# Two attention groups open their value sums with their own first product, not with a product of the zero tile

## The chip, the cores and the metric

The kernel runs on one core of one Trainium2 chip. The metric is the device time of one execution in microseconds. TensorE (PE in the profile, PEld for its weight loads) multiplies matrices into PSUM, which has eight banks of 128 x 512 float32; VectorE (DVE), ScalarE (ACT) and GpSimd (POOL) do the rest; SyncE (SP) issues most DMAs.

## The reference

A trunk of two layers over 1024 tokens of width 1024, in float32. Each layer projects the normalised input once, feeds the pieces to four groups of attention heads (A latent attention, B differential attention, C windowed attention with sinks, D attention over a neighbourhood of the token grid), joins their outputs, projects them, and adds an MLP with squared ReLU.

```
for l in range(DEPTH):                                  # 2
    h = rms_norm(x, norm1_g[l])
    proj = h @ w_in[l]
    (a_cq, a_ckv, a_kr, b_q, b_k, b_v, c_q, c_k, c_v, d_q, d_k, d_v) = jnp.split(proj, splits, axis=-1)
    y_a = mla_mixer(...)
    y_b = diff_mixer(...)
    y_c = swa_mixer(c_q, c_k, c_v, swa_sinks[l], cos64, sin64)
    y_d = na_mixer(d_q, d_k, d_v, na_rpb[l])
    mix = jnp.concatenate([rms_norm(y_a, out_g_mla[l]), y_b,
                           rms_norm(y_c, out_g_swa[l]), rms_norm(y_d, out_g_na[l])], axis=-1)
    x = x + mix @ w_out[l]
    h = rms_norm(x, norm2_g[l])
    x = x + jnp.square(jax.nn.relu(h @ w_up[l])) @ w_down[l]
return rms_norm(x, final_norm_g)
```

In C and D each query sees only keys nearby. With blocks of 128 tokens (in D the tokens are reordered so that this holds too), the queries of block i meet the keys of blocks i-1, i and i+1 only.

## The kernel before

**The order.** The program doesn't issue instructions as it goes. Every call adds a step to a list (`Plan.add`), and when all are there, `Plan.order` works out the order of each engine's queue: it walks through a model of the engines, and at each moment takes the step with the earliest due time whose inputs are ready and for which a buffer can be granted. Due times come from `Plan.stream`: each stage has a span in `SPAN` (D from 230 to 390, C from 300 to 405, B from 65 to 330, the latents' projections "lat" from 270 to 325 and "up" from 335 to 390), and the span is shared out among the stage's steps by the price of its TensorE steps. So the stages interleave: D and C run beside B and the projections. Steps added inside `together` form one unit and are issued one behind the other. All real instructions are emitted in one place, so the profile gives all of them line 677.

**Groups D and C.** Both use `banded` (1450), two calls per group and layer, each for two heads with 64 value columns each. For block i, `score` makes the scores of both heads (TensorE into banks "sb"), and `finish` turns them into exponentials (VectorE, ScalarE). For key block kb, `parts` (1469) transposes the probabilities of up to three query blocks into a bank "tr" and copies them to SBUF as `pt`. `products` (1486) multiplies values by `pt` into a bank "pv": head 0 into partitions 0 to 63, head 1 into partitions 64 to 127. One bank holds half of the queries, four blocks of 128 columns; a product covers the columns of those query blocks that the key block meets, so neighbouring products overlap in columns. The first half takes key blocks 1, 0 and later 4, 3, 2; the second takes 4, 3 and later 7, 6, 5. When a half is complete, `pair_out` (1244) copies it with one ScalarE instruction.

**The zero product.** Since no product covers the whole bank, `zeroed` (1481) opens each bank with one product of the zero tile: 128 x 128 zeros times a broadcast column of zeros, 512 columns wide, with `start=True`. All real products then add (`start=False`). `zeroed` is called twice per `banded`, so eight times per layer. It depends on nothing but a free bank. Groups A and B (`dense`, 1306) don't use it: there, products cover equal columns and the first one carries `start=True`.

The zero tile is also multiplied `IDLE` = 12 times at the very start, into a bank that nobody reads, and VectorE reads it as an operand in `softmax`.

Of the kernel before, what the change touches and what calls it, by code (L numbers as in the profile page):

```python
# [23 lines left out]
P = 128  # L24
# [612 lines left out]
class Trunk:  # L637
# [812 lines left out]
    def banded(self, qs, ks, vs, y, finish, grid=False):  # L1450


        nc = self.nc
        mm = nc.tensor.matmul
        heads = [slice(j * 64, j * 64 + 64) for j in range(2)]
        tiles, done = {}, {}

        def score(i):
            p = tiles[i] = self.ptile()
            lo, hi = max(i - 1, 0), min(i + 1, 7)  # L1460
            w, s0 = (hi - lo + 1) * P, (lo - i + 1) * P
            ps = [self.bank("sb")[:, :w] for _ in heads]
            for b, q, k in zip(ps, qs, ks):
                for n in range(2):
                    mm(b, q[:, i * P:(i + 1) * P], k[n][:, lo * P:(hi + 1) * P], start=n == 0, stop=n == 1)
            for j, b in enumerate(ps):
                finish(j, b, p[:, j * 512 + s0:j * 512 + s0 + w], i)

        def parts(kb):

            i0, i1 = max(kb - 1, 0), min(kb + 1, 7)
            out = []
            for j in range(2):
                t = self.bank("tr")
                for i in range(i0, i1 + 1):
                    at = j * 512 + (kb - i + 1) * P
                    nc.tensor.transpose(t[:, (i - i0) * P:(i - i0 + 1) * P], tiles[i][:, at:at + P], self.ident)
                out.append(self.transposed(t[:, :(i1 - i0 + 1) * P]))
            done[kb] = out, i0, i1

        def zeroed():
            pv = self.bank("pv")
            mm(pv, self.zero, self.zero[:, 0:1].broadcast_to([P, 512]), start=True, stop=False)
            return pv

        def products(pv, half, kbs):
            with self.plan.together():
                for kb in kbs:
                    pts, i0, i1 = done[kb]
                    q0, q1 = max(i0, half * 4), min(i1, half * 4 + 3) + 1  # L1490
                    for r, v, pt in zip(heads, vs, pts):
                        mm(pv[r, (q0 - half * 4) * P:(q1 - half * 4) * P], v[:, kb],
                           pt[:, (q0 - i0) * P:(q1 - i0) * P], start=False, stop=kb == 2 + 3 * half)

        for i in range(self.ahead):
            score(i)
        yield True
        for kb in range(8):
            if kb + self.ahead < 8:
                score(kb + self.ahead)  # L1500
            parts(kb)
            if kb == 1:
                pv = zeroed()
                products(pv, 0, (1, 0))
            if kb == 4:
                products(pv, 0, (4, 3, 2))
                self.pair_out(pv, y, 0, grid)
                pv = zeroed()
                products(pv, 1, (4, 3))
            yield True  # L1510
        products(pv, 1, (7, 6, 5))
        self.pair_out(pv, y, 1, grid)
        yield True
# [494 lines left out]
```

## Time and profile before

| | |
|---|---|
| median of 3 runs | 2522.7 us |
| lowest and highest run | 2518.65 and 2522.78 us |
| the profiled execution, its own time | 2517.78 us |
| its span, first to last instruction | 2516.0 us |
| mean granted TensorE clock | 0.996 |
| TensorE busy | 2467.4 us (98%) |
| VectorE busy | 1909.8 us (76%) |
| ScalarE busy | 1290.5 us (51%) |

Durations are microseconds unless marked ns. A row of the groups has engine, operation, output and inputs, shapes, count, then busy time in total, mean ns of one, and the idle time of the engine just before them with what ended it. A row of the timeline has start, duration, engine, line, operation, shapes and count; a bracket at its end is the idle time before it and what ended that. A row of the chain of waits has start, duration and what the time went to; "x334" is a run of 334 instructions with nothing between. Matmuls overlap in the pipeline and their ends are modelled, so the distance between starts says more than the duration. A row of the busy time by stages has the stage, its length, the busy time of PE, PEld, DVE, ACT and POOL with instruction counts, the granted clock, the DMA share and GB/s.

### The profile page before, as it was taken

How to read it: one execution, taken by the hardware profiler on the slowest of the kernel's cores; microseconds unless marked ns; L12 is line 12 of the kernel's file. 1: busy time of each engine (PE TensorE's matmuls, PEld its weight loads, DVE VectorE, ACT ScalarE, POOL GpSimd, SP SyncE). 2: the span in 40 equal slices, each digit the busy share in tenths (PEclk: the TensorE clock that was granted, in tenths of full speed). 3: DMA queues.
4: the chain of work that ended last, by engine and by line, in shares of the span. 5: the costliest groups of instructions: out<-in, count | busy, mean ns of one | idle time of the engine just before them, and what ended most of it. 6: DMA issues, size and time to landing. Idle time of an engine off the chain costs nothing.

```text
span 2516.0 us, 35396 instructions
## 1 busy us (share of the span) xinstructions
PE 2467.4 (98%) x12332; PEld 1967.1 (78%) x12332; DVE 1909.8 (76%) x3576; ACT 1290.5 (51%) x2397; POOL 379.7 (15%) x258
## 2 busy tenths in 40 slices
PE   8999999999999999999999999999999999999998
PEld 6777776778888887888877777677788888888887
DVE  7767867775877779888777677677678777898887
ACT  4545757653644445444425456666455444444454
POOL 3323224213000000000042231332140000000000
PEclk9999999999999999999999999999999999999999
DMA  5534478622244457444154344885123444665431
GB/s 180 180 112 133 122 218 234 197 80 72 78 165 159 151 202 271 147 142 139 72 182 130 119 117 135 232 255 170 46 70 117 155 155 158 231 231 158 130 105 67
DMA packets 190514, 378.56 MB, mean 150 GB/s; under 512 B 24112, under 2 KB 36352, under 8 KB 190336
## 3 DMA queue, kind: packets, MB, share of 16 engines
q1 hardware_dynamic: 175360, 350.09, 44.6%
q10 hardware_dynamic: 14976, 26.22, 2.7%
q8 instruction: 97, 1.59, 0.3%
q14 instruction: 81, 0.66, 0.1%
HBM read 260.15 MB, written 116.07 MB: 150 GB/s over the span
## 4 chain that ended last, share of the span: by engine, by line
PE 83%; DVE 8%; DMA 4%; ACT 2%; issue 2%; SPq 1%; POOL 0%; DVEq 0%; POOLq 0%; ACTq 0%
PE bank L677 83%; DVE p L677 2%; DVE part L677 1%; SPq L677 1%; ACT p L677 1%; DVE x L677 1%; DMA a<-in_w_down 1%; DVE sq L677 1%; DMA acts<-ev 1%; DVE col L677 0%; DMA latp<-lat 0%; DMA c<-in_w_down 0%; DVE xl L677 0%; DVE ev L677 0%; DVE both L677 0%
## 5 line engine op out<-in xcount | busy, mean ns | idle before, releaser
L677 PE MATMUL bank<-far,wh 128*128 128x512 f32 (+1 forms) x2848 | 870.3, 387 | 1.1 <-ACT wh L677 0.6
L677 PEld LDWEIGHTS bank<-far,wh 128*128 128x128 f32 x2848 | 532.4, 188 | 110.5 <-ACT wh L677 1.4
L677 PE MATMUL bank<-far,wl 128*128 128x512 f32 (+1 forms) x1424 | 550.3, 387 | 2.7 <-DVE wl L677 2.7
L677 ACT ACTIVATE p<-p,col 128x1024 f32<-128x1024 f32 (+2 forms) x320 | 294.6, 921 | 196.3 <-DVE col L677 194.2
L677 POOL TENSOR_TENSOR wl<-ws,wh 128x512 fp32r<-128x512 f32 (+1 forms) x138 | 191.1, 1390 | 1180.2 <-ACT wh L677 1089.8
L677 PEld LDWEIGHTS bank<-far,wl 128*128 128x128 f32 x1424 | 267.4, 188 | 57.9 <-DVE wl L677 3.4
L677 PE MATMUL bank<-stack 96*128 96x512 f32 (+2 forms) x896 | 285.0, 395 | 5.0 <-DVE col L677 2.3
L677 DVE TENSOR_TENSOR x<-bank,x 128x512 f32<-128x512 f32 (+1 forms) x276 | 187.2, 680 | 121.9 <-PE bank L677 121.0
L677 PE MATMUL bank<-ident,p 128*128 128x128 f32 x1376 | 253.6, 276 | 10.4 <-DVE part L677 4.8
L677 PE MATMUL bank<-xh,wh 128*128 128x512 f32 x608 | 250.9, 413 | 3.1 <-ACT wh L677 2.6
L677 PE MATMUL bank<-xh,wl 128*128 128x512 f32 x608 | 250.6, 413 | 1.1 <-POOL wl L677 1.1
L677 PE MATMUL bank<-xl,wh 128*128 128x512 f32 x608 | 250.6, 412 | 0.0
L677 PEld LDWEIGHTS bank<-ident,p 128*128 128x128 f32 x1376 | 171.3, 141 | 59.5 <-issue 10.7
L677 PEld LDWEIGHTS bank<-stack 96*128 96x128 f32 (+1 forms) x896 | 159.3, 189 | 43.8 <-DVE col L677 12.1
L677 ACT ACTIVATE pt<-bank 128x512 f32<-128x512 f32 (+2 forms) x256 | 137.5, 556 | 82.9 <-PE bank L677 75.2
L677 DVE TENSOR_TENSOR wl<-raw,wh 128x512 fp32r<-128x512 f32 x224 | 150.3, 690 | 34.5 <-ACT wh L677 34.0
L677 PE MATMUL bank<-pt,v 128*64 128x256 f32 (+2 forms) x1344 | 173.1, 396 | 2.2 <-ACT pt L677 2.0
L677 ACT ACTIVATE ev<-ev 128x512 f32<-128x512 f32 x128 | 80.6, 632 | 160.3 <-DVE ev L677 155.8
L677 DVE CUSTOM_DVE_ANT_0 p<-bank,zero,col 128x512 f32<-128x512 f32 x192 | 143.8, 749 | 22.2 <-PE bank L677 5.1
L677 PE MATMUL bank<-mix,wh 128*128 128x512 f32 x512 | 160.3, 393 | 0.0
L677 DVE CUSTOM_DVE_ANT_0 p<-bank,zero 128x512 f32<-128x512 f32 x192 | 131.7, 686 | 35.4 <-PE bank L677 34.1
L677 ACT ACTIVATE wh<-raw 128x512 fp32r<-128x512 f32 x224 | 135.4, 621 | 23.8 <-ACT ev L677 10.5
(158 smaller groups left out, 3904.5 us busy)
## 6 DMA issues: line engine op xcount, KB each, us to landing
act<-acts SPq DMA_DIRECT2D x224, 256.0 KB
raw<-in_w_up SPq DMA_DIRECT2D x128, 256.0 KB
acts<-ev SPq DMA_DIRECT2D x128, 256.0 KB
acts<-ev ACTq DMA_DIRECT2D x96, 256.0 KB
ws<-in_w_in SPq DMA_DIRECT2D x76, 256.0 KB
c<-in_w_down SPq DMA_DIRECT2D x64, 256.0 KB
rz<-drows SPq DMA_DIRECT2D x40, 256.0 KB
ws<-in_w_out SPq DMA_DIRECT2D x40, 256.0 KB
```

The lines of the kernel that those rows point to most:

```text
L677: getattr(s.eng.engine, s.op)(*[real(a) for a in s.args], **{k: real(a) for k, a in s.kw.items()})
```

## The change

`zeroed` goes. The bank is taken where it was called, and the first key block of each half (1 in the first half, 4 in the second) multiplies with `start=True`, once for each of the two heads. Columns of the bank that this first product does not cover are reached by later products with `start=False`.

```diff
-        def zeroed():
-            pv = self.bank("pv")
-            mm(pv, self.zero, self.zero[:, 0:1].broadcast_to([P, 512]), start=True, stop=False)
-            return pv
-
         def products(pv, half, kbs):
             with self.plan.together():
                 for kb in kbs:
                     pts, i0, i1 = done[kb]
                     q0, q1 = max(i0, half * 4), min(i1, half * 4 + 3) + 1
                     for r, v, pt in zip(heads, vs, pts):
                         mm(pv[r, (q0 - half * 4) * P:(q1 - half * 4) * P], v[:, kb],
-                           pt[:, (q0 - i0) * P:(q1 - i0) * P], start=False, stop=kb == 2 + 3 * half)
+                           pt[:, (q0 - i0) * P:(q1 - i0) * P], start=kb == 1 + 3 * half,
+                           stop=kb == 2 + 3 * half)
...
             if kb == 1:
-                pv = zeroed()
+                pv = self.bank("pv")
                 products(pv, 0, (1, 0))
             if kb == 4:
                 products(pv, 0, (4, 3, 2))
                 self.pair_out(pv, y, 0, grid)
-                pv = zeroed()
+                pv = self.bank("pv")
                 products(pv, 1, (4, 3))
```

## The prediction

> **What bounds the kernel now.** I read the page's busy shares first, then its chain of waits, then the groups by form, and last the timeline of TensorE around each product of the zero tile.
>
> ```profile
> span 2516.0 us, 35396 instructions
> PE 2467.4 (98%) x12332; PEld 1967.1 (78%) x12332; DVE 1909.8 (76%) x3576; ACT 1290.5 (51%) x2397; POOL 379.7 (15%) x258
> PE 83%; DVE 8%; DMA 4%; ACT 2%; issue 2%; SPq 1%; POOL 0%; DVEq 0%; POOLq 0%; ACTq 0%
> L677 PE MATMUL bank<-zero 128*128 128x512 f32 x28 | 12.3, 519 | 1.1 <-DVE pairs L677 1.1
> ```
>
> TensorE is busy for 98% of the span and carries 83% of the chain that ended last, so an instruction taken from its queue is worth its place in the queue, as long as the queue is what is late there. The fourth line is the group that the change touches: 28 products of the zero tile, of which 12 are the idle products at the start of layer 0 (`IDLE`), which stay, and 16 open the value sums of groups D and C. The 12.3 us are modelled ends and overlap with neighbours, so I don't use 519 ns as a price; I use the distance from one start to the next.
>
> Where is TensorE idle at all? The busy time by stages (columns: length, then busy time of PE, PEld, DVE, ACT, POOL) shows it. The first two lines are stages of layer 0 in which D and C run, the third and fourth are the same work in layer 1, the last is part of the MLP.
>
> ```profile
> 230.00:275.00 45.00, 42.14 (x224) 31.09 (x223) 43.01 (x106) 32.42 (x66) 15.19 (x11) 0.96 0.47 133
> 370.00:400.00 30.00, 26.69 (x170) 18.45 (x166) 20.71 (x52) 19.64 (x54) 16.00 (x11) 0.96 0.69 203
> 1470.00:1518.00 48.00, 43.89 (x234) 32.47 (x232) 46.16 (x109) 33.44 (x68) 16.81 (x11) 1.00 0.50 136
> 1613.00:1642.00 29.00, 27.05 (x177) 18.66 (x173) 19.61 (x55) 20.44 (x56) 17.46 (x12) 1.00 0.73 210
> 600.00:900.00 300.00, 300.00 (x1341) 248.94 (x1340) 238.19 (x359) 145.88 (x252) 21.26 (x14) 1.00 0.39 136
> ```
>
> Idle in the four stages: 2.86 + 3.31 + 4.11 + 1.95 = 12.2 us. In the MLP there is none, so what the attention gains or loses passes through to the end.
>
> **The change part by part.**
>
> *Sixteen products and their weight loads go.* Two per call of `banded`, two calls per group, two groups, two layers. In the timeline of TensorE they stand in three surroundings:
>
> ```profile
> 1562.76 0.39 PE L677 MATMUL bank<-xl,wh 128*128 128x512 f32 x1
> 1562.99 0.38 PE L677 MATMUL bank<-zero 128*128 128x512 f32 x1
> 1563.20 0.39 PE L677 MATMUL bank<-xh,wl 128*128 128x512 f32 x1
> ...
> 418.60 0.46 PE L677 MATMUL bank<-zero 128*128 128x512 f32 x1
> 418.90 0.38 PE L677 MATMUL bank<-ident,p 128*128 128x128 f32 x2
> 419.21 0.87 PE L677 MATMUL bank<-pt,v 128*64 128x256 f32 x8
> ...
> 439.31 0.46 PE L677 MATMUL bank<-zero 128*128 128x512 f32 x1
> 439.70 0.87 PE L677 MATMUL bank<-pt,v 128*64 128x256 f32 x8
> ```
>
> Eight stand between wide products and take 0.21 us each from start to start (1562.99 to 1563.20). Four follow transposes and take 0.30 (418.60 to 418.90). Four stand right ahead of their own group of 64-column products and take 0.39 to 0.41 (439.31 to 439.70). By start to start the sixteen are 8 x 0.21 + 4 x 0.30 + 4 x 0.40 = 4.5 us; that is the upper bound of what goes. The excess over 0.21 belongs to the neighbours, I think, and stays: two transposes that start at 418.90 are followed by a group of 64-column products 0.31 later without any zero product between. So I take 16 x 0.21 = 3.4 us, the row between plain products being nearest to the bare cost.
>
> [...]
>
> *Some of it lies in cover.* Four of the sixteen stand where TensorE waits soon after for something that isn't its own:
>
> ```profile
> 385.69 0.48 PE L677 MATMUL bank<-zero 128*128 128x512 f32 x1
> 386.10 1.78 PE L677 MATMUL bank<-pt,v 128*64 128x384 f32 x10
> 389.28 1.51 PE L677 MATMUL bank<-pt,v 128*64 128x128 f32 x10 [1.40 <-ACT pt L677]
> 390.72 0.72 PE L677 MATMUL bank<-latp,wh 128*128 128x512 f32 x2
> ...
> 391.52 0.38 PE L677 MATMUL bank<-zero 128*128 128x512 f32 x1
> ...
> 394.00 0.70 PE L677 MATMUL bank<-latp,wh 128*128 128x512 f32 x2 [1.08 <-DMA latp<-lat]
> ```
>
> The zero product at 385.69 is followed by a wait of 1.40 us for a copied block of probabilities, the one at 391.52 by 1.08 us for the latents that come back from memory. Both waits end when they end; TensorE merely waits 0.21 us longer. Layer 1 repeats this with two more. That takes 4 x 0.21 = 0.8 us off: 2.6 us stay. If the order moves them out of that cover, the whole 3.4 counts, or at most 4.5; if more of the others fall into one, the gain goes towards nothing.
>
> *The first product of a sum now opens it.* It is the same instruction with another flag. The groups A and B already open their sums with such a product, and the trace gives their products no other form than the ones that add. Bounds: zero below, since the widths stay; at most the 0.60 us below for each of sixteen, if it must wait where the zero product didn't. I take zero.
>
> *The bank is taken later.* Before, the zero product took the value bank 0.4 us (439.31 to 439.70) to 0.6 us (418.60 to 419.21) ahead of the first real product. Now the group itself must be granted the bank; what would hold it up is the copy of the sum before it, which ScalarE does in one instruction:
>
> ```profile
> 315.24 0.60 ACT L677 ACTIVATE y<-bank 128x512 f32<-128x512 f32 x1 [1.08 <-PE bank L677]
> ```
>
> No zero product here shows a wait of TensorE before it (its rows carry no bracket), so the banks were free in time; I take zero, with 16 x 0.60 = 9.6 us as the far end. Queued behind a waiting group would be everything on TensorE.
>
> *The order of everything is worked out again.* `Plan.order` places each instruction by its due time. A stream's due times are its span shared out by prices; without four products in D and four in C each remaining step of these streams shifts a little against B, the projections and the latents, whose due times stay. No step is added, no DMA is issued more or less, but SyncE's loads for D and C may change places with those of others. This is the largest unknown, and the trace has one row pair that sizes it. Layer 1 runs the same program as layer 0 from another starting state. The chain of waits has equal pieces in both:
>
> ```profile
> 308.28 56.76 PE bank L677 x334
> 383.65 3.02 DMA lat<-both
> 388.50 5.37 DMA latp<-lat
> 402.40 5.23 PE bank L677 x30
> ...
> 1552.20 56.76 PE bank L677 x334
> 1643.92 5.23 PE bank L677 x30
> ```
>
> From the 334-instruction piece to the 30-instruction piece layer 0 takes 402.40 - 308.28 = 94.12 us and layer 1 takes 1643.92 - 1552.20 = 91.72: a difference of 2.4 us from a slightly different order of the same work, in just the stretch where D, C and the latents meet. The pieces themselves agree to 0.01 us. So I take a re-ordering as worth up to 2.4 us either way in each layer, 4.8 in both, centred on nothing. Its bounds are the idle time of the stages above (12.2 us gained) and the loss in the second rival.
>
> *Sum.* -3.4 + 0.8 + 0 = -2.6 us. The profiled execution took 2517.78 us by its own clock, with 1.8 us around its span of 2516.0; it would become 2515.2. The median of the runs is 2522.7, 4.9 above the profiled one, so the forecast against the median is **2520.1 us**: a gain of 0.10%, inside the 0.2% (5.0 us) that I take as what a measurement of this kernel can tell from no change. With the order's 4.8 us either way the likeliest case runs from -5.0 to +2.2, that is 2517.7 to 2524.9.
>
> **The rivals.**
>
> *The order falls well (faster).* Layer 0's stretch takes layer 1's form, and layer 1's improves by as much: -2.6 - 4.8 = -7.4 us, 2515.3. It decides from 2.4 us of gain by order, half of that size. If all idle time of the four stages went too, -12.2 - 2.6 = -14.8, 2507.9. For it: there is idle time to win, and the products of D and C, which fill it, now have less in front of them. Against it: nothing in the change aims at those waits, and off TensorE the chain goes mostly through VectorE (8%) and DMAs (4%), which the change leaves as they are.
>
> *The latents' round trip loses its filler (slower).* From 383.65 to 394.00 the chain goes through the store and the load of the latents, 10.35 us, and TensorE is idle for only 3.3 us in this stage because products and transposes of D and C fill the rest. If these run ahead of the trip, since D's steps are now due differently, the filler is gone: 10.35 - 3.3 = 7.0 us more in layer 0, and 10.35 - 1.95 = 8.4 in layer 1 if its trip is as long. With all sixteen products saved that is 15.4 - 3.4 = +12.0 us, 2534.7. It decides from 8.4 us of lost filler in both layers together (5.0 + 3.4), a bit over half. For it: filler in that place is a matter of order alone. Against it: the shift of due times is small beside the length of the streams, and both layers kept the filler from different starting states.
>
> *The groups wait for their bank (slower).* The far end above, 9.6 - 3.4 = +6.2 us, 2528.9. It decides when nearly every group waits for a whole copy, which no row suggests.
>
> **How the numbers follow.** Forecast within 0.2%: 0.40. Order falls well by more than that: 0.35; the direct gain already goes half the way to the line. Lost filler: 0.18, bank waits and other mishaps of order: 0.07, together 0.25 for slower. The range goes from all idle time won (2507.9) to all filler lost (2534.7): 2508 to 2535.
>
> **What would show it.** Right: the group of zero products counts 12; TensorE's products number 16 fewer; no wait appears ahead of the 64-column groups; the distance from the 334-instruction piece to the end of attention shrinks by 1 to 2 us per layer; the MLP stages keep their length. Wrong on the order: the idle time of TensorE in the stages 230 to 275 and 370 to 400, or their like in layer 1, moves by more than 2.4 us. Wrong on the cover: the waits for the latents go or grow. Wrong on the price: attention stages whose idle time stays, yet whose length changes by other than 0.21 us for each product gone.

## The result and the profile after

The change is slower. Its median is 2527.6 us over 11 runs, against 2522.0 us over 11 runs of the kernel before: +5.6 us, ratio 1.0028 with a 95% interval of 1.0018 to 1.0038. The forecast was 2520.1 us, within 0.2%; the range of 2508 to 2535 held the time, the direction was missed (more than 0.2% slower had been given a chance of 0.25).

The profiled execution after took 2524.78 us by its own time, 7.0 more than the one before. Its page, the line of busy shares, the line of the chain of waits and the group of zero products:

```profile
span 2523.0 us, 35317 instructions
PE 2467.1 (98%) x12316; PEld 1966.1 (78%) x12316; DVE 1911.5 (76%) x3576; ACT 1290.8 (51%) x2397; POOL 379.9 (15%) x258
PE 82%; DVE 9%; DMA 5%; issue 2%; ACT 2%; SPq 1%; POOL 0%; DVEq 0%; POOLq 0%; ACTq 0%
L677 PE MATMUL bank<-zero 128*128 128x512 f32 x12 | 4.7, 574 | 1.1 <-DVE pairs L677 1.1
```

Sixteen products fewer (12316 for 12332), twelve zero products left: the edit did what it says. Yet the span is longer by 7.0 us. The chain of waits shows where, by the long pieces without a gap that both kernels have. First those of before, then those of after (start, duration, instructions in the piece):

```profile
92.45 132.81 PE bank L677 x700
961.11 279.34 PE bank L677 x1231
1326.81 136.13 PE bank L677 x718
2203.60 291.26 PE bank L677 x1299
```

```profile
91.31 132.82 PE bank L677 x700
964.22 279.36 PE bank L677 x1231
1329.53 136.13 PE bank L677 x718
2210.66 291.29 PE bank L677 x1299
```

The pieces themselves are equal to 0.03 us. From the first to the second, which spans the attention of layer 0 and the MLP up to its middle, after takes 872.91 us against 868.66: +4.25. From the third to the fourth, the same in layer 1, 881.13 against 876.79: +4.34. Between the second and third it gains 0.39 us, and the start was 1.14 us sooner. So both layers lose, and by the same amount, but not in the same way. The busy time over just these two stretches (length, PE, PEld, DVE, ACT, POOL busy, granted clock, DMA share, GB/s), before and then after; they hold the same work, less eight products in each:

```profile
92.45:961.11 868.66, 856.93 (x4469) 673.20 (x4470) 639.54 (x1276) 474.66 (x907) 156.27 (x106) 1.00 0.48 150
1326.81:2203.60 876.79, 864.46 (x4513) 679.19 (x4513) 645.00 (x1289) 479.18 (x915) 161.33 (x110) 1.00 0.48 150
```

```profile
91.31:964.22 872.91, 856.12 (x4461) 672.15 (x4461) 640.52 (x1276) 474.11 (x907) 156.96 (x106) 1.00 0.48 149
1329.53:2210.66 881.13, 867.07 (x4505) 681.06 (x4506) 645.59 (x1289) 479.88 (x915) 160.75 (x110) 0.99 0.48 149
```

In layer 0 TensorE is idle for 16.8 us instead of 11.7: waiting accounts for the whole loss. In layer 1 it is idle for 14.1 us instead of 12.3, and busy for 2.6 us longer with eight products fewer: there most of the loss is products that took longer, while the granted clock was lower (0.99 for 1.00).

Busy time by stages says where. Six stages, three of each layer's attention, make 660 us together; two of layer 1's aren't shown. They are fixed stretches of time, so they hold only nearly the same work before and after:

```profile
230.00:360.00 130.00, 127.01 (x715) 95.42 (x714) 101.19 (x258) 86.29 (x177) 25.92 (x18) 0.99 0.54 144
360.00:440.00 80.00, 73.67 (x455) 51.76 (x455) 56.42 (x146) 55.37 (x148) 38.16 (x25) 0.98 0.82 246
440.00:560.00 120.00, 119.55 (x804) 89.96 (x801) 90.04 (x209) 79.55 (x138) 23.78 (x14) 1.00 0.47 140
...
1604.00:1684.00 80.00, 74.96 (x477) 53.17 (x475) 56.52 (x152) 56.30 (x150) 39.54 (x26) 1.00 0.83 252
...
sum 660.00, PE 640.05 PEld 474.07 DVE 494.85 ACT 442.56 POOL 175.51; mean PE 106.67 PEld 79.01 DVE 82.48 ACT 73.76 POOL 29.25
```

```profile
230.00:360.00 130.00, 126.00 (x722) 95.61 (x722) 101.86 (x259) 86.98 (x180) 25.57 (x18) 1.00 0.55 148
360.00:440.00 80.00, 71.62 (x440) 50.19 (x439) 54.65 (x144) 53.62 (x145) 38.92 (x26) 0.96 0.77 236
440.00:560.00 120.00, 117.74 (x782) 87.19 (x780) 88.33 (x204) 78.53 (x136) 22.66 (x12) 1.00 0.49 140
...
1604.00:1684.00 80.00, 72.89 (x431) 51.87 (x430) 51.82 (x138) 51.86 (x138) 36.96 (x24) 0.91 0.75 232
...
sum 660.00, PE 633.19 PEld 468.64 DVE 489.25 ACT 438.14 POOL 172.94; mean PE 105.53 PEld 78.11 DVE 81.54 ACT 73.02 POOL 28.82
```

TensorE is idle for 26.8 us of the 660 after the change and for 20.0 before. The waiting is spread over several stages, and in one stage of layer 1 the granted clock falls from 1.00 to 0.91 besides.

### The profile page after: what moved, and what is told of

Its sections match the earlier page's. It is cut to its first block, busy times and chain, and to the rows that moved or that the text cites. A ratio compares the mean times of both kernels' runs of the same rounds, so it can differ in the third digit from the quotient of the medians.

```text
span 2523.0 us, 35317 instructions
## 1 busy us (share of the span) xinstructions
PE 2467.1 (98%) x12316; PEld 1966.1 (78%) x12316; DVE 1911.5 (76%) x3576; ACT 1290.8 (51%) x2397; POOL 379.9 (15%) x258
## 4 chain that ended last, share of the span: by engine, by line
PE 82%; DVE 9%; DMA 5%; issue 2%; ACT 2%; SPq 1%; POOL 0%; DVEq 0%; POOLq 0%; ACTq 0%
PE bank L677 82%; DVE p L677 3%; DVE part L677 1%; DMA stack<-qan 1%; DVE x L677 1%; DVE col L677 1%; DMA rz<-drows 1%; DMA acts<-ev 1%; SPq L677 1%; DMA a<-in_w_down 0%; DVE sq L677 0%; DMA c<-in_w_down 0%; ACT xh L677 0%; DVE mix L677 0%; ACT sq L677 0%
```

## The experiments

The order of the queues and the instructions themselves can be taken apart here, since the planner works on a list and the instructions are emitted afterwards. Theory: the products are worth what was forecast, and the new order costs more than that. Rival: the opening product itself is dear, or waits for its bank.

**Before's order, without the zero products.** The zero product is planned but not emitted, and the first products open the sums.

```diff
-            mm(pv, self.zero, self.zero[:, 0:1].broadcast_to([P, 512]), start=True, stop=False)
+            s = mm(pv, self.zero, self.zero[:, 0:1].broadcast_to([P, 512]), start=True, stop=False)
+            s.mark = 'planned only'
...
+                if s.mark == 'planned only':      # where all steps are emitted
+                    continue
```

> The order is worked out with the sixteen zero products in it, exactly as before, but they are not issued, and the first products open the sums as in the change: every queue stands as before, less sixteen entries on TensorE. Theory 'the new order costs it': the products themselves are worth the predicted 2.6 us (bounds 0 and 4.5), so this run is about 2.6 us faster than before, ratio 0.9990 (0.998 to 1.000), and some 8 us faster than the change. Rival 'the opening product costs it' (dearer in itself, or waiting for its bank): the order is as before, yet this run is slower than before by about the 5.6 us of the change, ratio 1.002.

Measured: 2519.2 us against 2521.0, ratio 0.9989 (0.9981 to 0.9998). That is 2.8 us faster, with 0.5 to 4.8 as the interval, where 2.6 was forecast. Opening a sum with its own product costs nothing that shows. This version is the fastest of all that ran, if only just clear of before.

The traces give the price product by product. Here is one place, before and in this run:

```profile
439.28 0.27 PE L677 MATMUL bank<-ident,col 128*16 128x128 f32 x1
439.31 0.46 PE L677 MATMUL bank<-zero 128*128 128x512 f32 x1
439.70 0.87 PE L677 MATMUL bank<-pt,v 128*64 128x256 f32 x8
```

```profile
438.82 0.27 PE L679 MATMUL bank<-ident,col 128*16 128x128 f32 x1
439.02 0.87 PE L679 MATMUL bank<-pt,v 128*64 128x256 f32 x8
```

From the transpose to the group of 64-column products it took 0.42 us with the zero product and takes 0.20 without: 0.22 is gone, though the zero product stood 0.39 ahead of the group. At eleven of the sixteen places the neighbours stand 0.21 to 0.22 us closer. At two (385.69 and its like in layer 1), right ahead of a group and of a wait, it is 0.40 and 0.41.

**The change's order, with the zero products.** One is emitted right ahead of each group, outside the plan.

```diff
+                if s.mark:                        # the first product of a sum; mark is its bank
+                    pv, zero = real(s.mark), self.zero.real()
+                    s.eng.engine.matmul(pv, zero, zero[:, 0:1].broadcast_to([P, 512]), start=True, stop=False)
```

> The order is worked out without zero products, exactly as in the change, but one is issued right ahead of each group's first product, which adds to it as before. Theory 'the new order costs it': slower than the change by what sixteen products are worth, 2.6 to 4.5 us, so 8 to 10 us above before, ratio about 1.0035. Rival 'the opening product costs it': back at the time of before, ratio 1.000.

Measured: 2529.3 us, ratio 1.0036 (1.0024 to 1.0049), 0.0008 above the change, or 2.0 us for sixteen products (-2.0 to 6.0, from the two intervals). In the trace the starts around them are 5.2 us further apart than after the change: ten products take 0.20 to 0.22 each, and the six that now stand between two groups of 64-column products take 0.51. The theory's side again; with its own instructions back, the kernel doesn't come back to the time of before. The rival is out: the order carries the loss. Between the first experiment and the change, which issue the same instructions, lie 1.0028 - 0.9989 = 0.0039, about 9.8 us of order alone (6.5 to 13.1).

The waits of TensorE by releaser show it too (total, times, longest). VectorE's small columns ("col": minima, reciprocals, running sums) are the largest or second in all four kernels; before, after, the first and the second experiment:

```profile
PE bank L677 <- DVE part L677: 10.0, 11, 2.7
PE bank L677 <- DVE col L677: 8.8, 13, 1.6
```

```profile
PE bank L677 <- DVE col L677: 14.4, 24, 2.0
PE bank L677 <- DVE part L677: 7.0, 5, 2.7
```

```profile
PE bank L679 <- DVE part L679: 9.3, 9, 2.6
PE bank L679 <- DVE col L679: 6.9, 11, 1.6
```

```profile
PE bank L680 <- DVE col L680: 14.4, 23, 2.0
PE bank L680 <- DVE part L680: 7.0, 5, 2.7
```

With the order of before TensorE waits 8.8 and 6.9 us for these columns, with the order of the change 14.4 and 14.4, whether the zero products are there or not. The waits for VectorE's tiles of 512 columns ("part") go the other way, from 10.0 and 9.3 to 7.0 and 7.0, and take back part of it. Over the whole span TensorE is idle for 48.6 and 45.1 us with the order of before (2516.0 less 2467.4, 2519.2 less 2474.1), for 55.9 and 56.1 with that of the change (2523.0 less 2467.1, 2531.5 less 2475.4). One of the places can be named. The transposes of 16 reciprocal columns (the denominators of C and D, 128*16) as a group, again in the order before, after, first, second experiment; the number behind the second bar is the idle time ahead of them:

```profile
L677 PE MATMUL bank<-ident,col 128*16 128x128 f32 x14 | 3.8, 273 | 2.9 <-DVE col L677 2.9
```

```profile
L677 PE MATMUL bank<-ident,col 128*16 128x128 f32 x14 | 4.0, 288 | 5.3 <-DVE col L677 5.3
```

```profile
L679 PE MATMUL bank<-ident,col 128*16 128x128 f32 x14 | 4.0, 288 | 1.7 <-DVE col L679 1.7
```

```profile
L680 PE MATMUL bank<-ident,col 128*16 128x128 f32 x14 | 3.9, 280 | 5.3 <-DVE col L680 5.3
```

and the longest wait for such a column in the timeline of TensorE after the change:

```profile
1646.88 0.38 PE L677 MATMUL bank<-ident,col 128*16 128x128 f32 x1 [2.04 <-DVE col L677]
1647.47 0.69 PE L677 MATMUL bank<-ident,p 128*128 128x128 f32 x2 [0.21 <-DVE pt L677]
```

The transpose stands in the queue before its reciprocals are done, and everything behind it waits 2.04 us. The planner places a step only when its model holds it ready, so in the model there is no wait here; orders that differ in such places look alike to it.

**Which part of the planning makes the new order?** Two things change in the plan: the due times of D and C, and the time and bank that a zero product takes. One kernel has the due times of before without the products, one the due times of the change with them.

```diff
# due times of before, products absent (the change, with this)
-        each, done = (end - start) / sum(cost), 0.0
+        gone = [n - first for n in self.gone if n >= first]
+        each, done = (end - start) / (sum(cost) + 512 / 2.4 * len(gone) + 14 * len(gone)), 0.0
...
+            done += (512 / 2.4 + 14) * gone.count(i)
# due times of the change, products there (before, with this)
-        cost = [s.cost[0] if s.eng.name == "tensor" else 1.0 for s in own]
+        cost = [0.0 if s.mark else s.cost[0] if s.eng.name == "tensor" else 1.0 for s in own]
```

> No zero products, but the due times of the steps of D and C are those of before (the price of the absent products is still counted when the spans are shared out). What differs from before in the planning is only that the products take no time and no bank. If the shifted due times are what costs: as fast as the first run, ratio 0.999. If the freed time and bank in the planner are enough to set off another order: anywhere between, within about 5 us of before; the same as the change (1.0025) if that is the sole cause.

> The zero products are planned and issued as before, but counted at no price when the spans are shared out, so D and C have the due times of the change. If the shifted due times are what costs: the new order's loss without the gain, about 8 us above before, ratio 1.0033. If they are not: as before, ratio 1.000.

Measured: 1.0027 (1.0017 to 1.0036) without products at the old due times, 1.0030 (1.0019 to 1.0042) with products at the new ones. Neither part is the sole cause: each by itself sets off another order, and each of these is as slow as the change's. Waiting explains less in these two: in their profiled executions TensorE is idle for 48.6 and 49.6 us of the span, only 3.5 and 1.0 more than with the order of before and the same instructions. What else makes them slow stays open.

**Is it the absence of the zero products, or any re-ordering?** Eight kernels move one span in `SPAN` by one unit, and nothing else: D or C, later or sooner, in the kernel before and in the change.

```diff
-    SPAN = {... "d": (230, 390), ... "c": (300, 405), ...}
+    SPAN = {... "d": (231, 391), ... "c": (300, 405), ...}    # or (229, 389); or c (301, 406), (299, 404)
```

> The kernel before with its zero products, and nothing changed but D's span, one unit later (231 to 391 for 230 to 390). The order of TensorE's queue comes out about as different from before as that of the change. Theory 'any re-ordering costs, because the order of before is a good one among many like it': slower than before by 0.2 to 0.4%, ratio 1.002 to 1.004. Rival 'what costs is the absence of the zero products from the planning': no loss here, ratio within 0.001 of 1.

> As the run before, with D's span one unit sooner (229 to 389). Theory of the good order: ratio 1.002 to 1.004. Rival: within 0.001 of 1.

> The change, with D's span one unit later (231 to 391). Theory of the good order: the change's order is an ordinary one, so another one without zero products lies around it, ratio 1.000 to 1.005, and may well beat it. Rival that the absence of zero products costs: at the change or above it, ratio 1.0025 or more.

> The change, with D's span one unit sooner (229 to 389). Theory of the good order: ratio 1.000 to 1.005, another draw. Rival: 1.0025 or more.

> The kernel before with its zero products, C's span one unit later (301 to 406 for 300 to 405). So far two nudged orders with zero products lie at 1.0008 and 1.0032, one with shifted due times at 1.0030. If orders planned with zero products are better as a class, and the change loses because it has none: this lies below 1.0015 (the nudges of D then were its upper part). If any re-ordering is a draw from one lot: 1.000 to 1.004, and over all nudges the mean of the kernels with zero products, less the 0.0011 that they cost, comes within 0.001 of the mean of those without.

> As the run before with C's span one unit sooner (299 to 404). Class theory: below 1.0015. One-lot theory: 1.000 to 1.004.

> The change with C's span one unit later (301 to 406). So far four orders planned without zero products lie at 1.0027 to 1.0034. Class theory: again 1.0025 to 1.0035. One-lot theory: 0.999 to 1.003, as wide a spread as with zero products.

> The change with C's span one unit sooner (299 to 404). Class theory: 1.0025 to 1.0035. One-lot theory: 0.999 to 1.003.

| span moved | with zero products | without |
|---|---|---|
| none | 1 | 1.0028 (1.0018 to 1.0038) |
| D one later | 1.0008 (0.9999 to 1.0017) | 1.0034 (1.0023 to 1.0045) |
| D one sooner | 1.0032 (1.0019 to 1.0045) | 1.0027 (1.0018 to 1.0036) |
| C one later | 1.0014 (1.0003 to 1.0024) | 1.0009 (1.0000 to 1.0018) |
| C one sooner | 1.0035 (1.0021 to 1.0048) | 1.0042 (1.0029 to 1.0054) |

A nudge of one unit, on a span of 105 or 160, costs the kernel before 0.08 to 0.35%, with no change to what is computed; the smallest, 1.0008, can't be told from nothing. No order tried is better than that of before; re-ordering it with the zero products kept costs 0.24% on average (the four nudges and the kernel with the shifted due times: 1.0008, 1.0032, 1.0014, 1.0035, 1.0030). Without zero products the six orders (the change, its four nudges, the one with the old due times) average 1.0028 and range from 1.0009 to 1.0042, which overlaps.

The two theories of these runs are not fully told apart. The theory that any re-ordering is a draw from one lot missed twice: 1.0008 lies below the 1.002 to 1.004 expected for D one later, and 1.0042 above the 0.999 to 1.003 expected for C one sooner in the change. A class of its own for kernels with zero products is contradicted by 1.0032 and 1.0035 on one side and by 1.0009 on the other. But the one-lot theory asked for means within 0.001, once the 0.0011 of the products is taken off, and they are 1.0013 and 1.0028: 0.0015 apart, about two standard errors of five and six such draws; over the nudges alone, as the expectation had it, they are 1.0011 and 1.0028. A small disadvantage of planning without the zero products may be there. That stays open.

## Why the prediction was wrong

- **The sixteen products.** Right. Forecast 2.6 us (bounds 0 to 4.5); taken out alone they gave 2.8 (0.5 to 4.8). The price of 0.21 us holds at eleven of the sixteen places, also ahead of 64-column groups, so the excess was mostly the neighbours', as assumed; it was the zero product's own where that stood between two such groups (0.51, second experiment). The four in cover are neither borne out nor refuted: the interval doesn't tell 2.6 from 3.4.
- **The first product opens the sum, and the bank comes later.** Right: nothing to pay. With the order unchanged the kernel is faster by the whole price, and in none of the four lists of waits does TensorE wait for ScalarE's copy of a sum (`y`). So the rival of groups that wait for their bank fell, and the far end of 9.6 us with it.
- **The order.** This is the step that failed. It was sized at up to 2.4 us per layer either way, "centred on nothing", from two passes of one program through the same stretch. Measured, it cost 9.8 us (6.5 to 13.1) where 4.8 was the most allowed for both layers, and none of the eleven other orders that ran has a lower ratio than that of before, with the same instructions on both sides. Two mistakes are in the step. The size: the row pair compared one order from two starting states, while the change makes another order, in both layers alike; D's and C's due times move by a fraction of their span, and a nudge of one unit in 160 can do nearly as much (1.0032 with D one sooner). The centre: an order that stands at the low end of its neighbours can't be re-drawn around itself; its neighbours lie 0.08 to 0.35% higher, and that would have been the middle to take. The trace of before doesn't show this; only the nudges do.
- **The rival of the latents' trip.** In layer 0 the loss is of its kind, waits that a filler no longer covers, but only a small part is in its place. The waits for the latents grew by 0.9 us only (1.6 to 2.5 over the whole span). TensorE's idle time went up in the stages at 360 to 440 (+2.1 us), 440 to 560 (+1.8) and 1604 to 1684 (+2.1). Over the whole span the waits for VectorE's columns rose by 5.6 us, those for its tiles of 512 columns fell by 3.0.
- **The rival of a good order.** No order without zero products is faster than before by 0.2%. The best version is the one that keeps the order.
- **"What would show it."** The sign for a wrong order did not appear where it was looked for. The four named stages after the change:

```profile
230.00:275.00 45.00, 41.22 (x226) 30.77 (x226) 42.93 (x105) 32.71 (x68) 16.82 (x12) 1.00 0.49 130
370.00:400.00 30.00, 26.14 (x163) 18.69 (x161) 20.53 (x54) 19.44 (x54) 14.67 (x10) 0.94 0.60 164
1470.00:1518.00 48.00, 45.92 (x238) 34.10 (x237) 45.90 (x112) 34.53 (x69) 17.83 (x12) 0.96 0.47 129
1613.00:1642.00 29.00, 27.12 (x149) 17.23 (x150) 16.66 (x50) 19.51 (x53) 15.63 (x9) 0.83 0.68 220
```

TensorE's idle time in them is 3.78, 3.86, 2.08 and 1.88 us, 11.6 together for 12.2 before, and none moved by 2.4. It grew by 6.9 over the six wider stages, outside these four. So the step also took the idle time of four stages for the place where an order shows. Of the other signs, the zero products count 12, TensorE's products number 16 fewer, the MLP pieces keep their length, and the waits for the latents grew.

How the loss divides between waiting and the clock is in part argued. For the two profiled executions: idle time grew by 5.1 and 1.7 us in the two stretches, 6.8 of the 7.0, and the products gone take about 2.6 off; so some 3 us are left for slower products. After the change layer 1's stretch has 17 us at half the clock (13.6 of them in the lines of the last section) and before's has none, while layer 0's has 6.8 both times. A row of sixteen 64-column products took 3.61 us at half the clock (1614.25 to 1617.86) and another row of the same form 1.88 at the full clock (1637.03 to 1638.91), so some 8 of the 17 us can be lost there (estimate from this pair), and this is enough. For the medians: within the runs of one kernel a mean clock lower by 0.001 goes with about 1.2 us more (estimate from the 174 runs whose clock is recorded), and the mean clock was 0.9915 over the runs of the change and 0.9939 over those of the first experiment. By that about 3 of the 9.8 us of order go with the clock and the rest with waits. No experiment here holds the clock fixed.

## What to carry to other kernels

Where a planner makes the order, an edit costs what its instructions cost plus what a new order costs, and on a queue that is 98% busy the second can be the larger: 9.8 us against 2.8 here. To judge the edit itself, apply it after the planning, so that the old order stays. And nudge an unrelated parameter by one unit, to see how far neighbouring orders lie from the present one, before sizing a change of order from its own trace.

## What was not expected of the hardware

The granted clock follows the order too, but not as the time does. On one chip the runs of the kernel before had mean clocks of 0.989 to 0.995 (23 runs); with D's span one unit later they had 0.994 to 0.997 (11 runs), and one unit sooner 0.989 to 0.991 (5 runs). All three issue the same instructions, and neither nudge is faster. In the 80 us from 1604 the clock of the profiled execution was 1.00 before and 0.91 after, and the kernel with before's order and without zero products had 0.94 there with less idle time (76.05 us busy of 80) than before:

```profile
1604.00:1684.00 80.00, 76.05 (x451) 53.73 (x452) 53.30 (x146) 53.45 (x144) 36.95 (x24) 0.94 0.81 244
```

So the sum of idle time doesn't set it. The 0.91 is made of stretches at half the clock. These are the three of that stage after the change, each behind the 3.4 us that went before it:

```profile
1609.15:1612.56 3.41, 2.27 (x17) 1.99 (x16) 2.08 (x6) 0.74 (x3) 1.96 (x2) 1.00 1.01 327
1612.56:1619.38 6.82, 6.13 (x25) 3.35 (x25) 3.93 (x12) 2.96 (x8) 5.23 (x4) 0.50 1.02 401
1629.62:1633.04 3.42, 1.92 (x14) 1.04 (x13) 3.38 (x13) 2.53 (x9) 2.39 (x2) 1.00 0.76 246
1633.04:1636.45 3.41, 3.41 (x12) 1.77 (x13) 0.75 (x1) 2.79 (x11) 3.41 (x2) 0.50 0.46 131
1643.28:1646.70 3.42, 1.57 (x14) 1.33 (x12) 3.25 (x6) 1.72 (x5) 2.44 (x2) 1.00 0.00 0
1646.70:1650.11 3.41, 3.02 (x12) 2.36 (x13) 2.96 (x9) 0.84 (x2) 1.37 (x2) 0.50 0.26 55
```

Of the stretches at half the clock that end inside the span, four before and six after last 3.41 us, and one, the first of these three, 6.82. In the 3.4 us ahead of these three TensorE was busy for 2.27, 1.92 and 1.57 us, 46 to 67% of it, so it was never wholly idle, and the longest single wait there, the one that ends at 1646.88, was 2.04 us. What brings the clock down is not shown.
